# Stacks of query and key parts made by ordinary matmuls with an identity instead of transpose-mode matmuls

## The chip, the core and the metric

The kernel runs on one core of a Trainium2 chip. The metric is the device time of one execution in microseconds (us); the number given for the kernel before is the median of three runs. One execution was also recorded by the hardware profiler, and all rows below come from that recording.

The core has five engines that work side by side, each through its own list of instructions in a fixed order: TensorE (PE) for matrix products, VectorE (DVE), ScalarE (ACT), GpSimd (POOL) and SyncE (SP), which here only starts transfers. An instruction waits until what it reads is there and until the buffer that it writes is free; everything behind it on the same engine waits with it.

## What is computed

The reference is a decoder trunk of two layers over 512 tokens with 1024 features, in float32. Each layer has three kinds of attention heads that share one input projection, and then a SwiGLU feed-forward part:

```
h = rms_norm(x);  p = h @ w_in                       # one projection, columns shared out
o_fox  = softmax(q k^T / 8 + c[t] - c[s]) v          # 6 forgetting heads of 64
o_diff = (softmax(q1 k1^T) - lam softmax(q2 k2^T)) v # 4 differential heads, q and k 2 x 32
score[t, s] = sum_h w[t, h] relu(qi[t, h] . ki[s])   # indexer, 4 heads of 64
sel = the topk best causal keys of each query by score
o_dsa  = softmax over sel of q k^T / 8, times v      # 6 sparse heads, one shared key and value
x = x + concat(o_fox, o_diff, o_dsa) @ w_out
x = x + (silu(gate) * up) @ w_down                   # gate, up = rms_norm(x) @ w_gate_up
```

All attention is causal. The kernel keeps the best 128 keys of each query (`topk` is a quarter of the 512 tokens) by a mask: keys that are not selected get a large bias.

## The kernel before

**Tiles.** Tokens go in four blocks of 128. Products that must be accurate are made from two parts of each operand, a high part rounded to float32r and the rest as a second float32r number; `mm3` multiplies high by high, low by high and high by low. A score of a forgetting or sparse head needs no `mm3`: the parts are laid next to each other along the feature axis, as [high | low], and a product over 128 rows has several of the terms at once. For that, the parts of queries and keys, which lie with tokens on the partitions, are turned round so that features lie on the partitions. This is what `stacked` does: it takes four blocks of [128 tokens, 128 part-features], turns each by one PE instruction with the 128x128 identity `identr` into a quarter of one PSUM tile `tp_...`, and lets ACT copy the tile to SBUF as `T_...`. In the instruction the block is the operand that is loaded into PE (a weight load, PEld in the trace), and the identity is the one that moves through.

There are 96 such stacks in the kernel, 48 in each layer, so 384 instructions: 4 indexer queries, 2 indexer keys and 2 shared keys (named `tp_iq`, `tp_ik`, `tp_sk`); 4 for each of the 4 differential heads (`tp_qd`, `tp_kd`); 3 for each of the 6 forgetting heads (`tp_qf`, `tp_kf`); 1 for each of the 6 sparse heads (`tp_qs`).

**Stages.** A layer begins with the projections and the indexer scores. Then the heads go through rounds: in round r the probabilities of head r are transposed (L450, tile `t_...`), head r + 1 is scored (L432, tile `s_...`), and head r - 1 weighs its values (L476, L482, L483, tile `o_...`), with units of projection work (L172 to L174, `mm3`, tile `pj`) laid between the stages. The differential heads come first, then the forgetting ones, then the sparse ones. Scores go from PSUM through a DVE reduction with the bias (L438, reads `s_...`, writes `x_...` and the row minimum `st_...`) and an ACT exponential (L439).

**The search.** Meanwhile DVE selects the best keys of each query: `top_keys` runs 16 rounds over three query blocks, and each round and block is a MAX (L831, the eight best of the row) and a MATCH_REPLACE (L832, which takes them out). These 96 steps per layer are called steps of the search below; three instructions (L835) turn the result into biases for the sparse heads. A tile `top0_3_8` is that of layer 0, block 3, round 8.

**What sets the order.** PE's order is that of the program text (the tables `ORDER`, `FILL` and `SEARCH` interleave the generators). The order of each other engine is set at build time by a scheduler, which keeps its own account of when each instruction could begin and picks among those that are ready by priority. Priorities come from the order of the text and are raised or lowered for some kinds of work by the table `AHEAD` (`"topk": 150` for the search, `"ttr": 1000` for the reductions of scores, `"stack": 60` for the copies out of the stacks). On the chip each engine then follows that fixed list.

**Buffers.** The PSUM tiles `tp_...`, `s_...`, `t_...` and a few small ones share four buffers (tag `st`). A PE instruction that writes such a tile waits until the reader of the tile that had this buffer four tiles earlier is through; for a score tile that reader is the DVE reduction L438.

Of the kernel before, what the change touches and what calls it, by code (L numbers as in the profile page):

```python
# [31 lines left out]
# Rounds of the heads: the order of the stages of each round; the units of projection work and the  # L32
# steps of the search for the best keys that follow each stage.
# [16 lines left out]
INDEX_FILL = "03210121000201021"  # units of projection work between the stages of the indexer  # L50
# by how much the scheduler prefers (or, below zero, puts off) a kind of work
# [6 lines left out]
# products of probabilities and values, for the pairs of the differential and forgetting heads and for  # L58
# the sparse heads: 4 in float32, 2 from parts
# [3 lines left out]
# Column chunks of the input projection: indexer queries; indexer key, shared key and value, gates;  # L63
# then query-key pairs and values of the differential and forgetting heads, and the sparse queries.
# [22 lines left out]
def trunk(ctx: ExitStack, tc: tile.TileContext, x_in, w_in, w_out, w_gu, w_dn, vecs, gfeat, rope, out):  # L87
# [21 lines left out]
    # ---- residual stream, feature-major: x[m][p, t] = x[t, 128 m + p]  # L109
# [4 lines left out]
    # ---- constants  # L114
# [6 lines left out]
    tri = const.tile([P, P], F32, name="tri")  # tri[s, t] = s <= t  # L121
    G.affine_select(out=tri, in_=ones, compare_op=ALU.is_ge, fill=0.0, base=0,
                    pattern=[[1, P]], channel_multiplier=-1)
    # causal[:, 384 - 128 i:] is the mask of query block i over its 128 (i + 1) keys
    causal = const.tile([P, S], F32, name="causal")
    cdiag = causal[:, S - P:]  # 0 where key <= query, else BIG
# [10 lines left out]
    # rope tables: [blk, 16] cos|cos, -sin|sin for 64-wide heads; [blk, 8] for 32-wide ones  # L137
# [5 lines left out]
    # values of a pair of heads and of the sparse heads: high | low  # L143
# [4 lines left out]
    # ---- weights: load, and split exactly into two 12-bit parts  # L148
    def weights(src, n, step, name, eng=V, load=None):
        """Parts (high, low) of n columns, as a function of the column slice."""  # L150
# [25 lines left out]
    def rsqrt(m, name, out=None):  # L176
        """m ** -0.5: a first value from the scalar engine, then a Newton step."""
        shape = list(m.shape)
        y = small.tile(shape, F32, tag="rs_y", name=f"rsy_{name}")
        t = small.tile(shape, F32, tag="rs_t", name=f"rst_{name}")  # L180
        A.activation(y, m, AF.Ln)
        A.activation(y, y, AF.Exp, scale=-0.5)
        e = V
        e.tensor_tensor(t, y, y, op=ALU.mult)
        e.tensor_tensor(t, t, m, op=ALU.mult)
        e.tensor_scalar(t, t, -0.5, 1.5, op0=ALU.mult, op1=ALU.add)
        e.tensor_tensor(out, t, y, op=ALU.mult)

    def split_input(l, which, ms):
        """Parts of x * g for feature tiles ms."""  # L190
# [12 lines left out]
    def square_sum(pool, name):  # L203
        """Sum over feature tiles of x * x."""
# [8 lines left out]
    def token_rms(acc, name):  # L213
        """1 / rms per token, token-major [P, NB]."""
# [9 lines left out]
    def attention(l, ap):  # L224
        """The attention half of layer l; on the tensor engine the stages of three heads overlap,
        with units of the projections in between."""
# [5 lines left out]
        # ---- small per-layer vectors  # L232
# [8 lines left out]
        # ---- projection of one chunk of columns, token-major  # L241
        def project(c, start=False):
            """Yields after each unit of the tensor engine's work; returns one [P, n] per token block.
            At the start a unit is a feature tile, not a token block."""
# [24 lines left out]
        # the first chunks go half by half, so that the last feature tiles of y may come late  # L269
        p_iq, p_ik, p_dq = project(C_IQ, l == 0), project(C_IK), project(C_DQK0)  # L270

        def step(gen, n):
            """n units of gen; what it returned, once it is through."""
            for _ in range(n):
                try:
                    next(gen)
                except StopIteration as e:
                    return e.value
# [36 lines left out]
        # ---- token-major inputs of the heads  # L315
        def head_norm(raw, nh, d, name):
            """raw [P, NB, nh, d] times 1 / rms over d, in place."""
# [23 lines left out]
        def split_hl(raw, hl, hi=False):  # L341
            """raw [P, NB, n, d] into hl [P, NB, n, 2, d]: high | low."""
# [3 lines left out]
        def split_hlh(raw, hl):  # L346
            """raw [P, NB, n, d] into hl [P, NB, n, 3, d]: high | low | high."""
# [4 lines left out]
        def split_values(src, dh, dl, b, mode):  # L352
            """Projected values of token block b into their parts."""
# [50 lines left out]
        # ---- stacks of transposes  # L404
        def stacked(src, name, tag="qk", bufs=5):
            """Transposes of src(b) [P, 128] for all token blocks, as one [128, S] tile."""
            ps = st_tile(f"tp_{name}", F32R)
            for b in range(NB):
                T.transpose(ps[:, b * P:(b + 1) * P], src(b), identr)
# [7 lines left out]
        def key_stacks(hl, name, tag="qk", bufs=5):  # L417
            """hl(b) [P, 3, 64] of a key head -> its [high; low] and [low; high] stacks."""
            return [stacked(lambda b: flat(hl(b))[:, 64 * e:64 * e + 128], f"{name}{e}", tag, bufs) for e in range(2)]

        # ---- scores, probabilities, weighted values of one head
        def scores(blocks, q, k, bias, p, stat, name):
            """Per query block: p = exp(logits - max), with the sums; q holds negated queries."""
# [17 lines left out]
        def transposed(blocks, p, parts, name, mode):  # L441
            """Probabilities of the query blocks, transposed into parts [keys, queries]."""
# [9 lines left out]
            for i in blocks:  # L452
                # key block j of query block i goes to POFF[j] + 128 (i - j)
# [16 lines left out]
        def weigh(js, o, parts, val, mode):  # L470
            """o += [high | low]^T P^T for key blocks js; the lower half is to be added to the upper one."""
# [15 lines left out]
        def broadcast_rows(cols, n, name):  # L487
            """cols [P, NB, n], token-major -> rows [n, S] in DRAM."""
# [10 lines left out]
        def out_parts(kt, osb, wide, name, g=None):  # L499
            """Parts of a pair's output osb times its rows, or times wide (token-major) and g (per feature)."""  # L500
# [13 lines left out]
        class Head:  # L514
            """One head of a pair. split, stack: its parts and their transposes; score, trans, pv by
            blocks; fin, oss, rows: the pair's output, after its second head."""
# [11 lines left out]
            def split_(self):  # L528
                pr, h = self.pr, self.h
                if self.kind == "d":  # L530
                    raw = raws["d", pr]
                    # queries high|high|low|low, keys high|low|high|low: one product has all four terms
# [48 lines left out]
            def biases(self, blocks):  # L581
                """What is added to the negated logits: the mask; for forgetting heads, the gates as well."""
# [15 lines left out]
            def score(self, blocks):  # L598
# [7 lines left out]
                else:  # L606
                    V.reciprocal(rr[self.pair][:, lo:hi, self.h], st[0][:, 4 + lo:4 + hi])
                    # p1 / s1 - lam p2 / s2 = (p1 - lam (s1 / s2) p2) / s1
# [57 lines left out]
            def row_factors(self):  # L666
                """The factors of both heads as rows over the tokens, on all partitions of a head."""
# [11 lines left out]
            def oss(self):  # L679
                """rms norm over each differential head's 64 features"""  # L680
# [24 lines left out]
        # ---- indexer, shared key and value, gates  # L705
# [19 lines left out]
        # gates: log sigmoid, cumulative sum over tokens  # L725
# [23 lines left out]
        # ---- what the tensor engine does between the stages of the heads  # L749
# [53 lines left out]
        # ---- indexer scores  # L803
# [8 lines left out]
        def index_score(h, q, i):  # L812
            """Adds head h to the scores of the causal keys; -BIG for the others."""
# [11 lines left out]
        def top_keys():  # L825
            """The TOPK best keys of each query: the others get the bias BIG."""
# [25 lines left out]
        # ---- the heads: in round r, head r is transposed, head r + 1 scored, head r - 1 weighs its values  # L852
# [34 lines left out]
    def feed_forward(l, fp):  # L887
# [4 lines left out]
        def gate_up(f, between=None):  # L892
            """The f-th tile of gate and up, before the norm."""
# [50 lines left out]
        for f in range(2, NF):  # L944
            activate(f, gate_up(f))
            # each group of the down projection follows once its inputs had time to arrive
# [7 lines left out]
    with tc.manual_schedule(engines={mybir.EngineType.PE}):  # L954
        # the tensor engine reaches its full clock while the first loads are under way
# [70 lines left out]
```

## Time and profile before

| | |
|---|---|
| median of three runs | 1309.02 us (1307.33 to 1311.05) |
| span of the profiled execution | 1310.7 us |
| PE busy | 1273.4 us, 97% of the span |
| PE weight loads (beside PE) | 1083.1 us |
| DVE busy | 809.8 us |
| ACT busy | 657.2 us |
| POOL busy | 245.0 us |
| mean granted clock of PE | 0.993 of full speed |

The profiled execution lies 1.7 us above the median. The layers' attention halves fill about 0 to 280 us and 690 to 930 us; the feed-forward halves follow each, and there PE hardly stops.

In a row of the timeline the columns are the start (us from the span's start), the duration in us, engine, line, operation, output and inputs, and shapes; "x4" means four instructions of that form in a row merged into one line, and a bracket at the end gives idle time before it and what ended that. Matmuls are pipelined: a row's duration is from entry to the end of the last result, and the next instruction starts long before. The time that one costs PE is the distance from its start to the next start.

### The profile page before, as it was taken

How to read it: one execution, taken by the hardware profiler on the slowest of the kernel's cores; microseconds unless marked ns; L12 is line 12 of the kernel's file. 1: busy time of each engine (PE TensorE's matmuls, PEld its weight loads, DVE VectorE, ACT ScalarE, POOL GpSimd, SP SyncE). 2: the span in 40 equal slices, each digit the busy share in tenths (PEclk: the TensorE clock that was granted, in tenths of full speed). 3: DMA queues.
4: the chain of work that ended last, by engine and by line, in shares of the span. 5: the costliest groups of instructions: out<-in, count | busy, mean ns of one | idle time of the engine just before them, and what ended most of it. 6: DMA issues, size and time to landing. Idle time of an engine off the chain costs nothing. (4 is left out here: it accounts for less than half of the span.)

```text
span 1310.7 us, 19466 instructions
## 1 busy us (share of the span) xinstructions
PE 1273.4 (97%) x7058; PEld 1083.1 (83%) x7058; DVE 809.8 (62%) x1833; ACT 657.2 (50%) x1514; POOL 245.0 (19%) x269
## 2 busy tenths in 40 slices
PE   9989999999999999999999899989899999999998
PEld 9988796777888888888899888968778888888887
DVE  5699996865444444444546999868745534544442
ACT  6668777854332233232456786768533323333321
POOL 2454464220000000000025535642100000000000
PEclk9999999999999999999999999999999999999999
DMA  5221121123333333333322212211323333333332
GB/s 182 88 90 42 53 81 36 59 81 97 98 97 97 97 97 89 97 95 98 93 86 82 73 50 65 62 53 54 94 88 97 97 97 97 97 90 107 95 93 99
DMA packets 35495, 112.62 MB, mean 86 GB/s; under 512 B 4024, under 2 KB 4552, under 8 KB 35400
## 3 DMA queue, kind: packets, MB, share of 16 engines
q1 hardware_dynamic: 35400, 111.38, 28.7%
q8 instruction: 56, 0.92, 0.3%
q14 instruction: 39, 0.32, 0.1%
HBM read 109.19 MB, written 2.17 MB: 85 GB/s over the span
## 5 line engine op out<-in xcount | busy, mean ns | idle before, releaser
L172 PE MATMUL gu<-yh,wh_gu 128*128 128x512 f32 x704 | 274.4, 390 | 3.3 <-DVE gs L909 3.3
L174 PE MATMUL gu<-yl,wh_gu 128*128 128x512 f32 x704 | 273.9, 389 | 0.0
L173 PE MATMUL gu<-yh,wl_gu 128*128 128x512 f32 x704 | 273.9, 389 | 0.0
L159 ACT ACTIVATE wh_gu<-raw_gu 128x512 fp32r<-128x512 f32 x176 | 111.2, 632 | 253.7 <-PE gu L174 211.8
L172 PE MATMUL pj<-wh_in,yh 128*128 128x256 f32 (+1 forms) x704 | 202.0, 287 | 0.7 <-ACT wh_in L159 0.7
L174 PE MATMUL pj<-wl_in,yh 128*128 128x256 f32 (+1 forms) x704 | 199.2, 283 | 0.2 <-DVE wl_in L162 0.2
L173 PE MATMUL pj<-wh_in,yl 128*128 128x256 f32 (+1 forms) x704 | 199.2, 283 | 0.2 <-DVE yl L199 0.2
L162 POOL TENSOR_TENSOR wl_in<-raw_in,wh_in 128x512 fp32r<-128x512 f32 x72 | 99.7, 1402 | 488.9 <-ACT wh_in L159 484.8
L162 DVE TENSOR_TENSOR wl_gu<-raw_gu,wh_gu 128x512 fp32r<-128x512 f32 x176 | 121.8, 692 | 109.4 <-ACT wh_gu L159 106.7
L172 PEld LDWEIGHTS gu<-yh,wh_gu 128*128 128x128 f32 x704 | 132.2, 188 | 31.0 <-DVE gs L909 3.7
L174 PEld LDWEIGHTS gu<-yl,wh_gu 128*128 128x128 f32 x704 | 132.1, 188 | 27.7
L173 PEld LDWEIGHTS gu<-yh,wl_gu 128*128 128x128 f32 x704 | 132.2, 188 | 27.2
L172 PE MATMUL dn<-gh,wh_dn 128*128 128x512 f32 x352 | 138.7, 394 | 0.0
L174 PE MATMUL dn<-gl,wh_dn 128*128 128x512 f32 x352 | 138.0, 392 | 0.0
L159 ACT ACTIVATE wh_dn<-raw_dn 128x512 fp32r<-128x512 f32 x96 | 57.3, 597 | 159.5 <-PE dn L174 111.5
L172 PEld LDWEIGHTS pj<-wh_in,yh 128*128 128x128 f32 x704 | 134.7, 191 | 2.6 <-issue 1.2
L173 PE MATMUL dn<-gh,wl_dn 128*128 128x512 f32 x352 | 136.6, 388 | 0.0
L173 PEld LDWEIGHTS pj<-wh_in,yl 128*128 128x128 f32 x704 | 135.0, 192 | 1.1 <-DVE yl L199 0.4
L174 PEld LDWEIGHTS pj<-wl_in,yh 128*128 128x128 f32 x704 | 135.1, 192 | 0.4 <-DVE wl_in L162 0.4
L162 DVE TENSOR_TENSOR wl_dn<-raw_dn,wh_dn 128x512 fp32r<-128x512 f32 x96 | 62.2, 648 | 68.5 <-ACT wh_dn L159 67.6
L174 PEld LDWEIGHTS dn<-gl,wh_dn 128*128 128x128 f32 x352 | 66.1, 188 | 15.5
L173 PEld LDWEIGHTS dn<-gh,wl_dn 128*128 128x128 f32 x352 | 66.1, 188 | 14.8
(301 smaller groups left out, 2153.8 us busy)
## 6 DMA issues: line engine op xcount, KB each, us to landing
raw_gu<-in_w_gu SPq DMA_DIRECT2D x88, 512.0 KB
raw_in<-in_w_in SPq DMA_DIRECT2D x39, 512.0 KB
raw_dn<-in_w_dn SPq DMA_DIRECT2D x32, 448.0 KB
raw_dn<-in_w_dn SPq DMA_DIRECT2D x16, 512.0 KB
cr<-rtd_c SPq DMA_DIRECT2D x12, 256.0 KB
raw_o_fox<-in_w_out SPq DMA_DIRECT2D x8, 384.0 KB
raw_o_dsa<-in_w_out SPq DMA_DIRECT2D x8, 384.0 KB
x<-in_x_in SPq DMA_DIRECT2D x8, 256.0 KB
```

Source lines behind the costliest of these rows:

```text
L159: A.activation(h[:, :w], raw[:, o:o + w], AF.Copy)
L162: eng.tensor_tensor(lo[:, :w], raw[:, o:o + w], f32(h[:, :w]), op=ALU.subtract)
L172: T.matmul(ps, ah, bh, start=first, stop=False, skip_group_check=True)
L173: T.matmul(ps, al, bh, start=False, stop=False, skip_group_check=True)
L174: T.matmul(ps, ah, bl, start=False, stop=last, skip_group_check=True)
```

## The change

In `stacked`, the four instructions are issued as matmuls of float32r operands with `start` and `stop` set instead of as transposes, and the PSUM tile is declared float32 instead of float32r. Operands, shapes, tile, buffers and the copy behind them are the same. A product of a block with an identity gives the block, turned round. Comments were removed from the text as well, and one blank line came in, so that lines from 410 on have a number larger by one.

```
         def stacked(src, name, tag="qk", bufs=5):
-            """Transposes of src(b) [P, 128] for all token blocks, as one [128, S] tile."""
-            ps = st_tile(f"tp_{name}", F32R)
+
+            ps = st_tile(f"tp_{name}")
             for b in range(NB):
-                T.transpose(ps[:, b * P:(b + 1) * P], src(b), identr)
+
+                T.matmul(ps[:, b * P:(b + 1) * P], src(b), identr, start=True, stop=True)
             dst = ap.tile([P, S], F32R, tag=tag, name=f"T_{name}", bufs=bufs)
```

PE's list has the same 6419 rows in the same order, 384 of them in the new form. The lists of the other engines hold the same instructions in another order: 278 of DVE's 1727 rows stand elsewhere, 134 of ACT's, 10 of POOL's and 4 of SP's. Most of what moved on DVE is the search.

DVE's list of the kernel before, at the first score reduction of the first forgetting head (`x_f0_0_00_0` is layer 0, pair 0, head 0, query block 0; MAX and MATCH_REPLACE are steps of the search):

```order
L831 MAX top0_3_8_2800<-sc0_3_687 128x8
L831 MAX top0_1_9_2817<-sc0_1_685 128x8
L832 MATCH_REPLACE sc0_3_687<-top0_3_8_2800,sc0_3_687 128x512
L832 MATCH_REPLACE sc0_1_685<-top0_1_9_2817,sc0_1_685 128x256
L831 MAX top0_2_9_2904<-sc0_2_686 128x8
L831 MAX top0_3_9_2907<-sc0_3_687 128x8
L438 ISA x_f0_0_00_0_2168,st_f0_0_00_2029<-s_f0_0_00_0_2163,fbf0_0_0_0_2146 128x128
```

The same place in DVE's list of the changed kernel:

```order
L832 MAX top0_2_12_3167<-sc0_2_686 128x8
L833 MATCH_REPLACE sc0_1_685<-top0_1_12_3164,sc0_1_685 128x256
L833 MATCH_REPLACE sc0_2_686<-top0_2_12_3167,sc0_2_686 128x384
L832 MAX top0_3_12_3173<-sc0_3_687 128x8
L832 MAX top0_1_13_3176<-sc0_1_685 128x8
L832 MAX top0_2_13_3179<-sc0_2_686 128x8
L833 MATCH_REPLACE sc0_3_687<-top0_3_12_3173,sc0_3_687 128x512
L439 ISA x_f0_0_00_0_2168,st_f0_0_00_2029<-s_f0_0_00_0_2163,fbf0_0_0_0_2146 128x128
```

Before, the search is in its round 9 when the reduction's turn comes, with 58 of the 96 steps done; now it is in round 13, with 80 done. In layer 1 the same two counts, 58 and 80, stand at `x_f1_0_00_0`.

DVE's list of the kernel before, at the first reduction of the next head, `x_f0_0_10_0` (`pt1` is the low part of transposed probabilities, `hk` and `ss` belong to the inputs of later heads):

```order
L832 MATCH_REPLACE sc0_3_687<-top0_3_11_3138,sc0_3_687 128x512
L831 MAX top0_1_12_3164<-sc0_1_685 128x8
L831 MAX top0_2_12_3167<-sc0_2_686 128x8
L832 MATCH_REPLACE sc0_1_685<-top0_1_12_3164,sc0_1_685 128x256
L832 MATCH_REPLACE sc0_2_686<-top0_2_12_3167,sc0_2_686 128x384
L325 TENSOR_REDUCE ss_f0_2_2355<-sq_f0_2_2_2359 128x8
L438 ISA x_f0_0_10_0_2384,st_f0_0_10_2289<-s_f0_0_10_0_2379,fbf0_0_1_0_2304 128x128
```

The same place in DVE's list of the changed kernel:

```order
L833 MATCH_REPLACE sc0_3_687<-top0_3_15_3247,sc0_3_687 128x512
L469 TENSOR_TENSOR pt1_f0_0_0_2271<-t_f0_0_0_2_2327,pt0_f0_0_0_2270 128x128
L836 TENSOR_SCALAR sc0_1_685<-sc0_1_685 128x256
L836 TENSOR_SCALAR sc0_2_686<-sc0_2_686 128x384
L836 TENSOR_SCALAR sc0_3_687<-sc0_3_687 128x512
L299 TENSOR_SCALAR gd1_7111<-vec1_6800 128x32
L300 COPY gd1_7111<-vec1_6800 128x32
L313 TENSOR_TENSOR nlam1_7124<-ls1_7119,le1_7122 128x1
L740 MEMSET before1_7749 128x6
L439 ISA x_f0_0_10_0_2384,st_f0_0_10_2289<-s_f0_0_10_0_2379,fbf0_0_1_0_2304 128x128
```

Here the count goes from 76 steps to all 96, and the three closing instructions of the search and four small ones have come ahead of the reduction as well. No instruction has moved from ahead of these two reductions to behind them.

On POOL, half of the low part of one weight chunk (`wl_in0_7_0`) now stands behind three instructions that it stood ahead of, which make biases of the first forgetting head (`fbf`). On ACT, copies that make the query parts of a differential head (L540) now stand ahead of the copy of a key stack (L412). On SP, the load of one weight chunk (`raw_in0_6_0`) now stands behind the loads of gate rows (`cr`).

## Rows read from the trace of the kernel before

**Rows 1.** Stretches: length; busy (count) of PE, PEld, DVE, ACT, POOL; PE clock; DMA:

```profile
68.00:190.00 122.00, 113.33 (x865) 102.17 (x865) 121.23 (x387) 91.98 (x263) 58.99 (x67) 0.99 0.21 66
719.00:811.50 92.50, 86.95 (x654) 77.38 (x653) 92.08 (x302) 72.66 (x205) 44.99 (x45) 0.98 0.21 62
```

**Rows 2.** Waits of DVE, 68 to 168 us: total us, times, longest:

```profile
DVE ss_f L325 <- ACT sq_f L323: 0.4, 1, 0.4
```

**Rows 3.** Timeline of DVE up to the first forgetting reduction (value loads left out):

```profile
145.90 1.01 DVE L831 MAX8 top<-sc 128x8 f32<-128x512 f32 x2
...
146.89 0.67 DVE L832 MATCH_REPLACE8 sc<-top,sc 128x512 f32<-128x512 f32 x1
...
147.56 0.40 DVE L832 MATCH_REPLACE8 sc<-top,sc 128x256 f32<-128x256 f32 x1
147.88 1.14 DVE L831 MAX8 top<-sc 128x8 f32<-128x384 f32 x2
148.94 0.27 DVE L438 CUSTOM_DVE_ANT_0 x_f<-s_f,fbf 128x128 f32<-128x128 f32 x1
```

**Rows 4.** Timeline of PE behind that reduction, layer 0 and layer 1:

```profile
149.61 0.62 PE L432 MATMUL s_f<-T_kf,T_qf 128*128 128x384 f32 x2 [1.21 <-DVE st_f L438]
...
798.08 0.62 PE L432 MATMUL s_f<-T_kf,T_qf 128*128 128x384 f32 x2 [1.22 <-DVE st_f L438]
```

**Rows 5.** Timeline of POOL and PE around one weight part that moves on POOL:

```profile
85.91 1.29 POOL L162 TENSOR_TENSOR wl_in<-raw_in,wh_in 128x512 fp32r<-128x512 f32 x1
...
87.61 0.86 POOL L590 TENSOR_SCALAR fbf<-cr,ncum 128x512 f32<-128x512 f32 x1
...
92.84 0.28 PE L174 MATMUL pj<-wl_in,yh 128*128 128x256 f32 x1
```

**Rows 6.** A weight load of `stacked` (ns min/median/max), and the timeline of twelve of its transposes:

```profile
L409 PEld LDWEIGHTS tp_ik<-identr,hlik x16: 138/140/143, 41.8 to 693.6; 128*128 128x128 f32 x16
...
41.87 0.80 PE L409 MATMUL tp_ik<-identr,hlik 128*128 128x128 f32 x8
42.50 0.50 PE L409 MATMUL tp_iq<-identr,hliq 128*128 128x128 f32 x4
42.84 0.35 PE L172 MATMUL pj<-wh_in,yh 128*128 128x256 f32 x1
43.03 0.28 PE L173 MATMUL pj<-wh_in,yl 128*128 128x256 f32 x1
```

**Rows 7.** Ordinary float32r products: load (busy us, mean ns), timeline of 202 moving columns:

```profile
L172 PEld LDWEIGHTS pj<-wh_in,yh 128*128 128x128 f32 x704 | 134.7, 191 | 2.6 <-issue 1.2
...
29.89 0.27 PE L174 MATMUL pj<-wl_in,yh 128*128 128x202 f32 x1
30.00 0.28 PE L172 MATMUL pj<-wh_in,yh 128*128 128x202 f32 x1
```

**Rows 8.** Timeline: a short float32r product, and eight plain float32 ones with their successor:

```profile
239.77 0.22 PE L482 MATMUL o_s<-pt_s,svals 128*128 128x128 f32 x1
239.83 0.22 PE L483 MATMUL o_s<-pt_s,svals 128*64 128x128 f32 x1
...
120.88 2.37 PE L476 MATMUL o_d<-pt_d,vals 128*64 128x512 f32 x8
123.18 0.33 PE L450 MATMUL t_d<-ident,p_d 128*128 128x128 f32 x1
```

**Rows 9.** Later waits of PE, layer 0 (168 to 280 us), layer 1 (811.5 to 930 us):

```profile
PE wo_dsa L172 <- ACT oh L510: 3.0, 1, 3.0
...
PE s_s L432 <- DVE st_s L438: 1.1, 1, 1.1
...
PE wo_dsa L172 <- ACT oh L510: 3.5, 1, 3.5
PE s_s L432 <- DVE st_s L438: 2.3, 1, 2.3
```

**Rows 10.** Stretch of PE at half clock behind a wait (columns as in rows 1):

```profile
151.78:155.19 3.41, 3.41 (x23) 3.41 (x21) 3.41 (x12) 2.72 (x8) 1.94 (x3) 0.50 0.00 0
```

## The prediction

> **What bounds the kernel now.** I began with busy time by stretch, then the waits, then the timeline at the places where a wait ends. Between 68 and 190 us, in the attention half of layer 0, the reader should see two engines close to full: PE busy for 113.33 of 122.00 us and DVE for 121.23; in layer 1 the same stage has DVE busy for 92.08 of 92.50 us [rows 1]. A full DVE need not be the bound, since a filler (the search) may be what fills it. The waits decide that: DVE has one wait of 0.4 us in a hundred microseconds [rows 2], while PE stops for DVE: the score product at 149.61 us waited 1.21 us for the score reduction L438 to release its buffer, and the one at 798.08 in layer 1 1.22 us [rows 4]. So here PE runs at DVE's pace, and what stands ahead of such a reduction in DVE's list delays PE, microsecond for microsecond. Outside these stages PE is the bound and stops seldom: after 168 us the long waits are for the outputs of sparse heads (3.0 and 3.5 us) and for a sparse score reduction (1.1 and 2.3 us) [rows 9].
>
> **Part 1: the product itself.** 384 transposes become ordinary products. A run of twelve goes from 41.87 to 42.84 us, 0.97 us, and the product behind it holds PE 0.19 us until 43.03 [rows 6] where such a product takes 0.11 to 0.12: with this 0.07 us the run costs 1.04 us, 0.087 us each. Their weight load takes 140 ns, that of an ordinary float32r product 191 [rows 6, 7]. The trace has no ordinary float32r product with 128 loaded and 128 moving columns. The nearest row is that with 202 moving columns: 29.89 to 30.00, 0.11 us from start to start [rows 7]; the load, not the 202 columns, should be what sets it, so I take 0.11 for 128 columns too: +0.024 us each. Bound below: a 128-column product that is followed by one with 64 loaded columns took 0.06 us [rows 8], which would be a gain of 0.025. Bound above: eight plain float32 products, two each with 512, 384, 256 and 128 moving and 64 loaded columns, took 2.30 us from 120.88 to 123.18 [rows 8], which is 0.115 us for every 128 moving columns; doubled for 128 loaded columns instead of 64, an estimate of 0.22 us, +0.13 each.
>
> 384 x 0.024 = 9.2 us of work on PE. What of it is on the path? Per layer 32 transposes stand before 68 us and 68 after 168 us, where PE is the bound; 92 stand in the stage that DVE bounds, where 8.7 us of PE are free [rows 1] and 92 x 0.024 = 2.2 us fits. So 2 x 100 x 0.024 = **+4.8 us**. With the cover gone it would be 4.4 more.
>
> A page of the Trainium skill speaks against the change: "Perfetto Trace Analysis", section Transposes, asks for transpose over a standard matmul, since a transpose skips arithmetic, and "TensorE: Matmul & The Clock Gate", section Terms, puts transpose mode at 4x faster for FP32. By that an ordinary product would cost 4 x 0.087 = 0.35 us, and 200 of them on the path +52 us, about 1383 with part 2 (an estimate). No run here shows the ordinary form on these operands; the row of 0.11 us, on float32r operands, does not agree with it.
>
> **Part 2: DVE's order.** The diff touches PE alone, but the lists of the other engines come out in another order, and DVE's is the one that matters. Ahead of the reduction of the first forgetting head stand 80 steps of the search where 58 stood, in both layers, and nothing has moved out from ahead of it. Price of a step: from 145.90 to 148.94 us DVE does six, with their value loads, and nothing else (two MAX, two MATCH_REPLACE, two MAX), 3.04 us, 0.507 each [rows 3]. 22 x 0.507 = 11.1 us. DVE has no idle time ahead of that reduction to take them in (the wait of 0.4 us comes later, for an L325 behind it) [rows 1, 2], so it begins at about 160.0 instead of 148.94, and the product that waits for it has no slack: it already waits 1.21 us [rows 4]. PE therefore resumes 11.1 us later, in layer 1 as well (wait 1.22) [rows 4].
>
> Is it given back? At the next head's reduction all 96 steps stand ahead where it was 76: 20 x 0.507 = 10.1 us, with seven small instructions behind them, so DVE is still that late. Behind it DVE no longer has any search to do and is early; but PE then has to do all its remaining work, which is as much as before, and can only regain what it waited. Those waits follow PE's own products (scores, then reduction, exponential, transpose; sparse outputs at the end) and move with them. So nothing comes back, and the term is 2 x 11.1 = **+22.3 us**.
>
> **Part 3: other lists.** On POOL, half of a low weight part goes behind three instructions that make forgetting biases. It ran at 85.91 for 1.29 us, the longest of the three takes 0.86 us (at 87.61), and PE needs it at 92.84 [rows 5]: 5.6 us of room cover at most 3 x 0.86 = 2.6 us; if the room were gone, 2.6 us would be the price. On SP one weight load goes behind the loads of gate rows; its parts are due still later, and the same 5.6 us bounds what a late chunk could be worth. On ACT two copies of query parts go ahead of a key stack; the score behind it would be late by about a microsecond, but its reduction stands behind the longer list on DVE, and this is hidden there. I take zero, with up to 3 us in the range. PSUM's tile type changes nothing in bytes or buffers.
>
> The sum against the profiled execution: 1310.7 + 22.3 + 4.8 = 1337.8 us of span; the median stands 1.7 us lower, so **1336**.
>
> **The clock.** Behind the wait at 149.61 PE was granted 0.50 of full speed, 1.2 instead of 2.4 GHz, for 3.41 us, with PE busy all through [rows 10]. A stretch of that kind loses about 1.7 us. Longer or additional waits in the same stage may bring one or two more per layer: up to 2 x 2 x 1.7 = 6.8 us, which I keep for the upper end, not in the sum. The wait that is there now brings one already.
>
> **Rivals.**
>
> *The moved search is absorbed.* If PE had work in hand that doesn't depend on DVE, or if DVE's list before held the same steps elsewhere ahead of the reduction, only the products would count: 4.8 to 9.2 us, 1314 to 1318. It decides at the wait before 149.61: if PE waits no longer there, this holds. Against it: PE follows the text's order and cannot pull anything forward, and the wait is already above zero [rows 4].
>
> *Faster: the search's early end takes waits away.* DVE would be free from about 180 us on, and the waits that PE now has later, 3.0 + 1.1 + 3.5 + 2.3 = 9.9 us [rows 9], would vanish, while the moved steps cost nothing: 1309.0 + 4.8 - 9.9 = 1304. It needs the reduction at 148.94 to start no later than now; from there on each step ahead of it eats a half microsecond of the gain, so some ten steps per layer decide. Against it: 22 steps stand there, and the two longest of these waits are for ACT.
>
> *An ordinary product costs as a plain float32 one.* +0.13 x 200 = 26 us on the path, and 92 x 0.13 = 12 us per layer in the DVE stage, over the 8.7 us of room by 3.3: 1309.0 + 22.3 + 26 + up to 6.6 = 1357 to 1364. For it: the upper bound; against it: the operands are float32r, as in [rows 7].
>
> *The change does nothing on PE* (the product is carried out as before, 0.087 us each): the order on DVE is still the new one, 1331.
>
> **How the numbers follow.** Forecast 72%: with product costs from -0.01 to +0.05, some give-back (up to 2 us per layer) and up to four more stretches at 1.2 GHz it spans 1327 to 1347. Absorbed, wholly or by half (to 1320): 12%. Faster rival 3%. Plain float32 price 5%. Nothing on PE 2%. Further stalls beyond 1347 (DVE against POOL, ACT's two copies): 6%. The range from 1318 to 1347 leaves out most of the absorbed case, the faster one, the float32 price and the stalls, about 20%. A measurement of this kernel tells 0.3% (3.9 us) from no change: faster 3%; within it 4% (absorbed, with products at their cheap end); slower 93%.
>
> **What would show it.** In the changed kernel's trace: weight loads of `stacked` near 190 ns rather than 140 and 0.11 us from start to start; PE's busy sum up by about 9 us; the first forgetting reduction at about 160 us instead of 148.94, in layer 1 the same shift; a wait of PE for `st_f` or `st_d` L438 several microseconds longer between 95 and 170 us, or several such waits that add up to 11; DVE without gaps until then, the search over near 170 to 180 us, and idle time of DVE behind it. The lists of PE's work after 280 us should take as long as before. I am wrong if that reduction comes no later than 152 us, if PE has regained its lag by 280 us, or if the products cost other than 0.06 to 0.22 us.

## The result and the profile after

The changed kernel takes **1338.47 us** (median of 4 runs, 1337.61 to 1341.57) where the kernel before took 1310.03 in the same comparison: a ratio of **1.0227** (95% interval 1.0203 to 1.0250). The two medians are 28 us apart (their quotient is 1.0217); by the ratio, which the table below goes by, the loss is 30 us. The forecast was 1336, in a range from 1318 to 1347. The time is where it was said to be; the experiments show that two terms of the sum were not what they seemed, and that the close agreement is partly luck.

The page of the changed kernel, span and engines, beside 1310.7 us, PE 1273.4 and DVE 809.8 before (this profiled execution is the slowest of the four, 3.1 us above the median):

```profile
span 1339.8 us, 19460 instructions
PE 1296.9 (97%) x7058; PEld 1101.7 (82%) x7058; DVE 806.0 (60%) x1833; ACT 658.9 (49%) x1514; POOL 236.8 (18%) x269
```

The span grew by 29.1 us. PE's busy time grew by 23.5 us and its idle time (span less busy) from 37.3 to 42.9, by 5.6. That is the first surprise: a delay by DVE ought to stand in PE's idle time.

First the products. A weight load of `stacked`, and twelve of the new products in the timeline of PE (start, duration):

```profile
L410 PEld LDWEIGHTS tp_kf<-identr,hk_f x96: 186/192/192, 153.7 to 889.7; 128*128 128x128 f32 x96
...
42.98 1.00 PE L410 MATMUL tp_ik<-identr,hlik 128*128 128x128 f32 x8
43.82 0.61 PE L410 MATMUL tp_iq<-identr,hliq 128*128 128x128 f32 x4
44.27 0.33 PE L172 MATMUL pj<-wh_in,yh 128*128 128x256 f32 x1
44.44 0.28 PE L173 MATMUL pj<-wh_in,yl 128*128 128x256 f32 x1
```

The load went from 140 to 192 ns. Twelve products take 1.29 us, where twelve transposes took 0.97 [rows 6]. The product behind them holds PE 0.17 us (44.27 to 44.44) where such a product takes 0.12; with these 0.05 us the run costs 1.34 us, 0.112 each, against 0.087 for a transpose. So +0.025 us each, where +0.024 was forecast from a row with 202 columns.

Then DVE's timeline up to the first reduction of a forgetting head, in layer 0 and in layer 1, and the PE product that waits for it in layer 0:

```profile
159.35 0.67 DVE L833 MATCH_REPLACE8 sc<-top,sc 128x512 f32<-128x512 f32 x1
159.95 0.28 DVE L439 CUSTOM_DVE_ANT_0 x_f<-s_f,fbf 128x128 f32<-128x128 f32 x1
...
825.31 0.27 DVE L439 CUSTOM_DVE_ANT_0 x_f<-s_f,fbf 128x128 f32<-128x128 f32 x1
...
160.63 0.44 PE L433 MATMUL s_f<-T_kf,T_qf 128*128 128x384 f32 x1 [0.42 <-DVE st_f L439]
```

The reduction begins at 159.95 instead of 148.94 [rows 3], 11.0 us later, and the product at 160.63 instead of 149.61 [rows 4], 11.0 later too. PE's lag, the start of a product here less the start of the same product before, is 14.0 us at the end of layer 0's attention half (292.10 before, 306.10 now), and 27 to 29 from 827 us to the end of layer 1's: nothing is given back. But the product's wait has not grown; it fell from 1.21 to 0.42 us. Where PE's lag went instead, the stretches of the first stage show (columns as in rows 1; 102.39 to 109.22 and 805.50 to 815.70 lie ahead of those two reductions):

```profile
68.00:190.00 122.00, 110.48 (x782) 98.10 (x782) 116.29 (x380) 83.75 (x237) 52.78 (x61) 0.94 0.20 59
719.00:811.50 92.50, 82.94 (x588) 73.76 (x587) 82.52 (x266) 66.17 (x186) 35.91 (x36) 0.95 0.20 60
...
102.39:109.22 6.83, 5.12 (x23) 5.13 (x24) 6.65 (x28) 4.46 (x17) 0.07 (x1) 0.50 0.00 0
805.50:815.70 10.20, 9.45 (x33) 6.93 (x34) 8.24 (x33) 6.11 (x19) 0.83 (x1) 0.50 0.00 1
```

PE was granted 1.2 instead of 2.4 GHz in eleven stretches of 3.41 us (37.5 us) where the kernel before had five (17.1 us, one of them [rows 10]); a stretch that begins in the last 2 us of either span is left out. At half clock a projection product of 256 columns takes 0.21 us from start to start, at full clock 0.12:

```profile
105.01 0.41 PE L174 MATMUL pj<-wl_in,yh 128*128 128x256 f32 x1
105.22 0.41 PE L172 MATMUL pj<-wh_in,yh 128*128 128x256 f32 x1
```

The longer work fills time in which PE would have waited; this is my reading, not shown by itself, and not all of it: in the run search_back below, with five such stretches as before, PE's busy time still grew by 13.7 us (to 1287.1) and its idle time by 1.8. In the changed kernel 20 us more at half clock account for up to 10 us of the 23.5 us by which PE got busier (an estimate), the products for 384 x 0.024 = 9.2 us; the remaining 4 are not assigned. DVE, gapless before [rows 1, 2], now has gaps: from the first step of the search to the first forgetting reduction it idles 4.0 us, before it was 0.2. Its longest waits from 68 to 160 us:

```profile
DVE x_d L439 <- PE s_d L433: 2.0, 1, 2.0
DVE raw_d L339 <- POOL rb_d L338: 1.5, 1, 1.5
```

DVE waits for PE (this wait ends at 111.36 us, behind the first two stretches at half clock), and for a rope part on POOL.

### The profile page after: what moved, and what is told of

Its sections match the earlier page's. It is cut to its first block, busy times and chain, and to the rows that moved or that the text cites. A ratio compares the mean times of both kernels' runs of the same rounds, so it can differ in the third digit from the quotient of the medians.

```text
span 1339.8 us, 19460 instructions
## 1 busy us (share of the span) xinstructions
PE 1296.9 (97%) x7058; PEld 1101.7 (82%) x7058; DVE 806.0 (60%) x1833; ACT 658.9 (49%) x1514; POOL 236.8 (18%) x269
## 4 chain that ended last, share of the span: by engine, by line
PE 75%; DVE 15%; DMA 4%; ACT 3%; issue 2%; POOL 1%; SPq 0%; DVEq 0%; ACTq 0%; POOLq 0%
PE gu L172 12%; PE gu L173 12%; PE gu L174 12%; PE dn L172 6%; PE dn L174 6%; PE dn L173 6%; PE pj L172 4%; PE pj L173 4%; PE pj L174 4%; DVE sc L833 3%; DVE top L832 3%; DMA rw_s<-rtd_s 2%; DVE x_d L439 1%; DMA rw_f<-rtd_f 1%; PE wo_dsa L172 1%
## 5 line engine op out<-in xcount | busy, mean ns | idle before, releaser
L172 PE MATMUL pj<-wh_in,yh 128*128 128x256 f32 (+1 forms) x704 | 205.0, 291 | 0.6 <-ACT wh_in L159 0.6
L173 PE MATMUL pj<-wh_in,yl 128*128 128x256 f32 (+1 forms) x704 | 201.9, 287 | 0.0
L162 POOL TENSOR_TENSOR wl_in<-raw_in,wh_in 128x512 fp32r<-128x512 f32 x72 | 96.6, 1357 | 512.7 <-ACT wh_in L159 486.7
L172 PEld LDWEIGHTS pj<-wh_in,yh 128*128 128x128 f32 x704 | 138.2, 196 | 2.5 <-issue 1.2
L173 PEld LDWEIGHTS pj<-wh_in,yl 128*128 128x128 f32 x704 | 138.4, 197 | 0.7
L174 PEld LDWEIGHTS pj<-wl_in,yh 128*128 128x128 f32 x704 | 137.9, 196 | 0.2 <-DVE wl_in L162 0.2
```

The source lines that it names most:

```text
L162: eng.tensor_tensor(lo[:, :w], raw[:, o:o + w], f32(h[:, :w]), op=ALU.subtract)
L172: T.matmul(ps, ah, bh, start=first, stop=False, skip_group_check=True)
L173: T.matmul(ps, al, bh, start=False, stop=False, skip_group_check=True)
L174: T.matmul(ps, ah, bl, start=False, stop=last, skip_group_check=True)
```

## The experiments

The lists of the four other engines can be set apart from the products. In the runs below every instruction of DVE, ACT, POOL and SP is tied behind its neighbour in a chosen list, with an order-only edge (issue order, no wait; lines of these kernels are numbered 4 higher than in the kernel before, so that L436 there is L432). With the transposes and the lists of the kernel before, this gives the same program as before, instruction for instruction. The edit, the same in all twelve runs but for the table `QUEUES` and for whether `stacked` has transposes or products:

```
                 feed_forward(l, fp)
+    traced = {i.name: i for i in tc.nc.cur_bb.bb.instructions}
+    for queue in QUEUES:                     # one list of instruction numbers for each engine
+        seen = [f"I-{k}" for k in queue if f"I-{k}" in traced]
+        for earlier, later in zip(seen, seen[1:]):
+            tc.add_manual_dep(traced[later], earlier, mybir.DependencyInfo(
+                mybir.DependencyClass.NoSync, mybir.DependencyReason.DATA), reason="order")
```

The theory was that of the prediction: the moved search makes the loss. What was measured, all against the kernel before on the same chip; "lists" says whose order the engines follow, "reduction" is the start of the first forgetting reduction in layer 0 in the profiled execution, "at 1.2" the number of 3.41-us stretches of PE at half clock:

| run | products | search | other DVE, ACT | POOL, SP | ratio (95% interval) | us | reduction | at 1.2 |
|---|---|---|---|---|---|---|---|---|
| kernel before | no | old | old | old | 1 | 0 | 148.94 | 5 |
| changed kernel | yes | new | new | new | 1.0227 (1.0203 to 1.0250) | +30 | 159.95 | 11 |
| products_old_lists | yes | old | old | old | 0.9982 (0.9967 to 0.9997) | -2 | 148.24 | 3 |
| the same again | yes | old | old | old | 0.9993 (0.9979 to 1.0007) | -1 | 151.87 | 3 |
| transposes_new_lists | no | new | new | new | 1.0175 (1.0147 to 1.0202) | +23 | 157.93 | 11 |
| search_alone2 | no | new | old | old | 1.0208 (1.0187 to 1.0230) | +27 | 160.64 | 13 |
| search_half | no | half | old | old | 1.0095 (1.0075 to 1.0115) | +12 | 155.69 | 8 |
| search_back | yes | old | new | new | 1.0158 (1.0136 to 1.0180) | +21 | 154.15 | 5 |
| dve_act_rest_new | yes | old | new | old | 1.0131 (1.0095 to 1.0166) | +17 | 151.11 | 7 |
| pool_sp_new | yes | old | old | new | 1.0031 (1.0015 to 1.0047) | +4 | 150.91 | 5 |

(us: ratio less one, times 1310.)

### Products or order

> Ordinary products as in the changed kernel, but DVE, ACT, POOL and SP issue in exactly the order of the kernel before. Theory (the moved search makes the loss): only the products on the path are left, +4.8 us, 1313 to 1318; the first forgetting reduction stays within 2 us of 148.9. Rival (the products themselves make most of the loss, by their loads, their time or the clock): at least 1325. Rival (ordinary products cost nothing beside the load): 1309.

> Transposes as before, but DVE, ACT, POOL and SP issue in exactly the order of the changed kernel. Theory: +22.3 us, 1329 to 1335, the first forgetting reduction at about 160 instead of 148.9. Rival (the products make the loss): below 1315. Together with the run of ordinary products under the old lists it should add up to the whole loss of 28 us; if both are small, the two parts need each other.

The products under the old lists cost nothing: -2 us, and -1 when the run was repeated. The new lists with the old transposes cost 23 us, within a microsecond of the term in the prediction (22.3). So the loss is the order, which the scheduler chose anew because of the products; the products alone would have been free. The two do not add up to the whole: products cost -1 to -2 us under the old lists and, by the two ratios, about 7 under the new ones (0.5%, each ratio known to 0.25%). Under the new lists both variants have eleven stretches at half clock, and PE's busy time differs by 9.7 us (1287.2 and 1296.9), about the 9.2 us of the products, while its idle time differs by 2 (44.9 and 42.9): little hides them there. Under the old lists PE's busy time grew by 4.3 us in the first run (1277.7 against 1273.4) and by 8.0 in the repeat (1281.4), and its idle time fell from 37.3 to 29.6 and 30.7. So most of the added work went into waits that were there anyway. Both runs had three stretches at half clock instead of five, which by the estimate above gives back up to 3.4 us; how much of the products' low cost comes from that, no run separates.

### The search by itself

> Transposes as before and all lists as before, except that the steps of the search stand as far ahead in DVE's list as in the changed kernel (80 instead of 58 ahead of the first forgetting reduction). Theory: the same as with all new lists, within 4 us, 1328 to 1335. Rival (the moves on ACT, POOL and SP, or of other DVE instructions, carry it): below 1320.

It took 1.0265 (1.0237 to 1.0293), +35 us, more than with all new lists. The trace shows that the run was not what it was meant to be: the first step of the search began at 82.95 us instead of 68.22, since the list let no step start before all twelve score updates were through, and then the steps stood packed ahead of early reductions. PE waited longer for score reductions than in any other run:

```profile
PE s_d L436 <- DVE st_d L442: 25.5, 6, 8.6
```

So it tells only that packed steps cost more. The same with that mended, and with half the distance:

> Transposes and all lists as before, only the steps of the search stand where they stand in the changed kernel relative to the other DVE instructions (31 instead of 24, 58 instead of 40 and 80 instead of 58 ahead of three reductions); other than in the first try of this, a step may start as soon as the scores of its own query block are complete, as in both kernels, so that the search begins at 68 us and not at 83. Theory: as with all new lists, 18 to 27 us above the kernel before. Rival (the first try's 35 us are the true price of the search, and other moves in the new lists win a part back): 30 to 37 us above. Rival (the other moves carry the loss): less than 10 above.

> As the run before, but each step of the search moves only half as far (69 instead of 58 or 80 ahead of the first forgetting reduction). Theory (PE runs at DVE's pace with no slack, 0.5 us a step): half of that run's loss, 9 to 14 us above the kernel before. Rival (a threshold: some steps fit in without loss): less than 6. Rival (the loss comes from the clock that falls at any longer wait): nearly all of it, above 16.

22 steps cost 27 us in the two layers, 11 steps 12 us: proportional, 0.6 us for a step that DVE takes 0.5 us for [rows 3]. Neither slack nor a threshold shows. At half the distance the reduction stands between the two ends:

```profile
155.69 0.28 DVE L442 CUSTOM_DVE_ANT_0 x_f<-s_f,fbf 128x128 f32<-128x128 f32 x1
```

### The search put back

> The changed kernel with ordinary products and its lists for ACT, POOL, SP and all of DVE except that the steps of the search are put back to where they stand in the kernel before (58 ahead of the first forgetting reduction). Theory: the loss is gone, -4 to +5 us against the kernel before. Rival (the other moves or the products carry a good part under these lists): 10 us or more above.

This is where the theory failed. With the search back at 58 steps the loss is still 21 us. The waits of PE between 60 and 170 us in that run:

```profile
PE s_d L436 <- DVE st_d L442: 2.7, 1, 2.7
PE t_d L454 <- DVE p_d L626: 1.9, 1, 1.9
PE s_d L436 <- ACT T_kd L416: 1.1, 1, 1.1
```

The second is new: PE waits for a combination of probabilities of a differential head (`p_d`, L622 of the kernel before). DVE's timeline there, first before, then with the search put back, and POOL's in the latter:

```profile
92.39 0.34 DVE L611 SCALAR_TENSOR_TENSOR st_d<-st_d,nlam,st_d 128x1 f32<-128x1 f32 x2
92.65 1.27 DVE L622 SCALAR_TENSOR_TENSOR p_d<-p_d,st_d,p_d 128x384 f32<-128x384 f32 x2
```

```profile
94.42 1.20 DVE L615 SCALAR_TENSOR_TENSOR st_d<-st_d,nlam,st_d 128x1 f32<-128x1 f32 x2
95.55 2.36 DVE L626 SCALAR_TENSOR_TENSOR p_d<-p_d,st_d,p_d 128x384 f32<-128x384 f32 x2
```

```profile
94.18 1.44 POOL L546 TENSOR_TENSOR hq_d<-raw_d,hq_d 128x256 fp32r<-128x256 f32 x2 [2.67 <-ACT hq_d L544]
95.56 1.28 POOL L166 TENSOR_TENSOR wl_in<-raw_in,wh_in 128x512 fp32r<-128x512 f32 x1
```

The same four instructions take 3.5 us (94.42 to 97.91) instead of 1.5 (92.39 to 93.92), because under the new lists they meet two TENSOR_TENSORs of POOL (the last part of this section returns to such meetings). Ahead of that DVE had waited 1.11 us at 87.05 for a rope part on POOL (`raw_d`, L343, waiting for `rb_d`), whose addition stands four score reductions earlier in DVE's new list. Two more runs split what is left:

> Ordinary products, the search where it stands in the kernel before, POOL and SP with the lists of before; ACT and the rest of DVE with the lists of the changed kernel. The run with all new lists but the old search lost 20 us, which the theory of the search alone does not explain. New theory (small changes of order among head inputs and combinations on DVE and ACT delay the transposes of probabilities that PE waits for at 93 and 744 us): the 20 us are all here, 16 to 24 above the kernel before. Rival (the moved weight part on POOL and the moved load on SP): less than 6 above.

> Ordinary products and DVE and ACT with the lists of before; POOL and SP with the lists of the changed kernel. Theory (DVE and ACT carry it): as with the products under the old lists, -4 to +4 against the kernel before. Rival (POOL's list holds up DVE or a weight part): 8 or more above.

ACT and the rest of DVE carry +17 us, POOL and SP +4; against the products under the old lists (-2) that is 19 and 6, 25 together, about the 23 that the search put back still lost. In the last one DVE's instructions other than the search took 52.0 us instead of 50.2 from the first step to the reduction, and DVE idled 1.1 instead of 0.2, and PE waited 1.12 us at a place where it had not waited at all:

```profile
106.48 0.66 PE L413 MATMUL tp_qd<-identr,hq_d 128*128 128x128 f32 x4 [1.12 <-DVE st_d L442]
```

Behind it PE ran at 1.2 GHz from 108.5 to 112 us. ACT's list and the rest of DVE's were not tried apart, so which instruction of the two carries most of the 17 us is open.

So three edits of the lists, each alone, cost 27 us (with transposes), 19 and 6 (with products), and all together 23 with transposes and 32 with products: far less than their sum of 52. No run has the transposes with the other new lists and the old search, so a part of the 19 and 6 may be the products, which cost 8 to 9 us more under all new lists than under the old ones. The reading that fits is that they delay the same reductions, so that a longer delay covers part of the others. PE's lag bears it out in layer 0. At the product that begins at 103.61 us before (the first of a `tp_qd`) the lag is 7.9 us in the changed kernel, 4.5 with the search alone, 5.9 with the search put back; at the score product of 149.61 it is 11.0, 11.7 and 5.2. (Each of these has 1.1 to 1.3 us in it that are there at 10 us.) Between the two the moved search by itself adds 7.2 us, but only 3.1 in the changed kernel, which the other lists had already made late.

### Putting the search off

> Transposes and lists as before, except that the search is put off: 49 instead of 58 steps ahead of the first forgetting reduction, 20 instead of 24 and 34 instead of 40 ahead of two earlier ones, the last steps among the instructions ahead of the sparse heads. Theory (PE runs at DVE's pace there, and the search sets it): PE's waits for score reductions between 68 and 168 us (2.4, 1.2, 0.6 us) and their like in layer 1 shrink, 1299 to 1305. Rival (these waits are latency and not DVE's list): 1307 to 1311. Rival (the steps that are left push later reductions): above 1312.

1.0016 (1.0001 to 1.0031), no gain. The reduction did come 2.4 us earlier, at 146.56, and in layer 1 3.3 earlier (794.13 against 797.40). The gain was lost behind 168 us, where the steps put off stand ahead of work for the sparse heads; PE's waits there, of which the second is new:

```profile
PE wo_dsa L176 <- ACT oh L514: 2.9, 1, 2.9
PE rt_f L494 <- ACT sq_s L327: 2.4, 1, 2.4
PE t_f L454 <- ACT p_f L443: 2.0, 2, 1.9
```

> Ordinary products with the lists of before, and a tenth of the search's steps put off (52 instead of 58 ahead of the first forgetting reduction), the last ones into idle stretches of DVE ahead of one late forgetting reduction and of one output product (195 and 214 to 218 us). Theory: the gain of the earlier try (the first forgetting reduction 2.4 us earlier, in layer 1 3.3) without what it lost behind 190 us, together with the products under the old lists: 5 to 9 us below the kernel before. Rival (the waits only move to the next place): 1 to 4 below, as with the products alone.

1.0013 (1.0001 to 1.0026): no gain either, against the kernel before or against the products alone (0.9982 and 0.9993). The reduction came at 149.62, after a search that began at 69.94. Neither of the two later places of the search gained anything.

### Small instructions beside POOL

What is left is why DVE needed less time for the same other instructions in the changed kernel. From the first step of the search to the first forgetting reduction DVE spent, by its rows:

| | search | other 171 | idle | began | reduction |
|---|---|---|---|---|---|
| before, layer 0 | 29.3 | 51.2 | 0.2 | 68.2 | 148.9 |
| changed, layer 0 | 40.1 | 45.8 | 4.0 | 70.0 | 159.9 |
| before, layer 1 | 29.4 | 48.4 | 0.2 | 719.4 | 797.4 |
| changed, layer 1 | 40.2 | 46.2 | 4.8 | 734.1 | 825.3 |

The search cost 10.9 us more, as forecast (11.1); the other instructions cost 5.4 and 2.2 less. To see by how much an instruction was late, I take its time (start to next start) less that of the same instruction where it meets no TENSOR_TENSOR of POOL, in seven of the traces. In layer 0 of the kernel before, eleven took over 0.3 us more, 9.5 us in all, and every one of them began while POOL ran a TENSOR_TENSOR; in the changed kernel there were four, 3.3 us. All that began so, small excesses too, add up to 9.5 and 4.0 us, in layer 1 to 6.6 and 4.1: differences of 5.5 and 2.4 where 5.4 and 2.2 are to be explained. One of the eleven, with the POOL instruction that it met (before; duration in the second column):

```profile
140.43 0.99 DVE L184 TENSOR_TENSOR rst_d<-rsy_d 128x8 f32<-128x8 f32 x1
...
138.40 3.00 POOL L162 TENSOR_TENSOR wl_in<-raw_in,wh_in 128x512 fp32r<-128x512 f32 x2 [8.37 <-ACT wh_in L159]
```

An instruction on 128x8 elements, 0.16 us elsewhere, lasts 0.99 and ends at 141.42, when the second of the two POOL instructions in its row ends (138.40 + 3.00 = 141.40). The page "SBUF — State Buffer" of the Trainium skill, section "SBUF: two separate sides", says that DVE and GpSimd share one pair of ports, which an instruction holds to its end, and that a DVE instruction with two inputs in SBUF needs it while GpSimd reads there; the trace agrees (0.99 us, ended 0.02 us behind POOL).

> Ordinary products with all lists of before, but on DVE eight small instructions (four in each layer, of 0.07 us where nothing else runs), which took 0.4 to 1.2 us because they began while POOL ran a TENSOR_TENSOR and ended when that ended, change places with the one to three steps of the search behind them. Theory (a step of the search does not wait for POOL, such an instruction does): they fall to at most 0.2 us, the other instructions of DVE ahead of the first forgetting reduction take 2 to 4 us less in each layer, the reduction comes 1.5 to 3.5 us earlier, and PE regains what it waits for DVE there, 1 to 4 us in all. Rival (POOL delays whatever DVE runs beside it): the time of the search grows by as much. Rival (the stalls move to the next instruction): nothing changes.

> The same kernel as the first run (ordinary products, all lists of before), beside the run with the small instructions moved. Theory: again 0 to 4 us below the kernel before; the stretches at 1.2 GHz are again fewer than the five of the kernel before if the products are what keeps the clock up, about five if their number was chance.

Eight such instructions, four in each layer, took 6.8 us in all under the old lists and 3.7 with one to three steps of the search moved ahead of them (four of them still 0.6 to 0.9 us each). The same instruction as above, with ordinary products in both kernels (first with the lists of before, then moved):

```profile
143.34 0.99 DVE L188 TENSOR_TENSOR rst_d<-rsy_d 128x8 f32<-128x8 f32 x1
```

```profile
141.42 0.16 DVE L188 TENSOR_TENSOR rst_d<-rsy_d 128x8 f32<-128x8 f32 x1
```

The time of the search stayed at 29.3 us: its steps do not wait for POOL. The gain per layer was smaller than expected, though (the other instructions 1.9 us less in layer 0, 0.4 in layer 1), because some met the next POOL instruction. The kernel takes 0.9981 (0.9965 to 0.9997) of the kernel before, 2.5 us less; against the same kernel without the move (0.9993, 0.9979 to 1.0007) it is not told apart. The repeat of the first run had three stretches at half clock again.

## Why the prediction was right, and where it was not

**The order of the search: right in its place, near in its size.** DVE's list sets the pace, the reduction begins 11.0 us later where 11.1 was forecast, a step of the search costs about half a microsecond, and half the steps cost half. With transposes all new lists cost 23 us where the sum had 22.3, but the search by itself costs 27 (24 to 30 by its interval).

**But the 11 us are not made only of search steps.** In layer 0 they are +10.9 for the steps, -5.4 for fewer meetings with POOL, +3.8 of new gaps on DVE, and +1.8 of lag that PE brought from before 68 us (1.1 of it is there at 10 us, ahead of the first stack; the 32 products make about 0.8); in layer 1 +10.8, -2.2, +4.6 and 14.7 of lag, 27.9 together. The step that failed is that what stands ahead of such a reduction in DVE's list delays PE "microsecond for microsecond": DVE's list had no idle time, but its instructions had 9.5 us of hidden waiting in them, counted as busy. And 7.9 of the 11.0 us of PE's lag were there at 103.61 us already, 5.9 with the search put back. The tight agreement is partly luck.

**The products: right price, wrong path.** +0.024 us each was right. That 200 of them lie bare on the path, +4.8 us, was not: under the old lists they cost nothing (-2 and -1 us). PE's waits in the whole span, before and then with products under the old lists (engine line <- engine line: us in all, times, longest):

```profile
PE s_d L432 <- DVE st_d L438: 4.0, 4, 2.1
PE s_s L432 <- DVE st_s L438: 3.4, 2, 2.3
PE t_f L450 <- ACT p_f L439: 3.3, 4, 1.5
```

```profile
PE s_d L436 <- DVE st_d L442: 2.6, 4, 1.0
PE s_s L436 <- DVE st_s L442: 2.3, 2, 1.2
PE t_f L454 <- ACT p_f L443: 1.5, 4, 0.6
```

They shrank by 4.3 us in all: PE arrived later, and others were no later. So PE also waits where I took it for the bound. Under the new lists the same products cost about 7 us. By the rule of "TensorE: Matmul & The Clock Gate", section Terms, in the Trainium skill, transpose mode is 4x faster for FP32; on these float32r operands the runs show 0.087 against 0.11 us, 1.3 times and not 4.

**The other lists: zero was wrong, and hidden.** I looked at a weight part on POOL, a load and two copies, and found cover for each. What I passed over were moves among head inputs on DVE and ACT (a rope addition ahead of four reductions is one), 19 us with the products and the old search, and POOL's instructions as something that small ones of DVE run into, 6 us with SP's. Which moves carry most of the 19 is open: three moves were weighed, where 134 of ACT's rows stand elsewhere. In the changed kernel their cost is hard to see, because the search delays many of the same reductions; DVE's new gaps (1.5 us for the rope part alone) are a trace of it. The bound of 3 us for them was off by a factor of five or more (25 us, or 16 without what the products may have in it); the rival with the search absorbed would not have given 1314 but some 1331 (1.0158 times 1310).

**The clock.** I kept up to four more stretches at 1.2 GHz for the upper end; there were six more. They also undo one of the signs that I named: PE's waits for DVE did not grow by 11 us (between 68 and 170 us from 5.9 to 7.6), which I put down to PE's work at half clock. A lag is better read from the starts of the same instruction in both traces than from the waits.

**Nothing comes back: right.** The lag of 11.0 us at the first forgetting reduction is 14.0 at the end of the layer's attention half. The rival in which an early search frees DVE for later is out: the search ends at 174 us, and from 168 to 300 us PE's wait for a sparse score reduction fell from 1.1 to 0.3 us, but waits for `pt_f` and `pt_s` on DVE came instead (1.2 and 0.5), and the longest, for ACT's sparse outputs, went from 3.0 to 3.2.

## What to carry to other kernels

A change to one instruction can be free and still cost 2%, when a scheduler orders other engines anew because of it: compare the lists of every engine, and look for what now stands ahead of the instruction that the bound engine waits for. Then pin the old order and run the change without the reordering; it tells in one run which of the two to mend. And when two edits delay the same instruction, taking one away shows the other: price each alone before calling one the cause.

## What the runs showed of the hardware

A DVE instruction of 0.15 to 0.21 us (`rst_d` and `om_d` on 128x8, `ss_f` on 128x16, `st_d` on 128x2) lasted up to 1.3 us when it began beside a POOL TENSOR_TENSOR, and ended 0.01 to 0.03 us behind POOL's (141.42 against 141.40 above). Not every instruction does: in the kernel before, 2 RECIPROCALs, 3 TENSOR_REDUCEs and 16 score reductions ahead of the first forgetting reductions of both layers began beside one with at least 0.5 us to go and were not stretched; MAX and MATCH_REPLACE did not stretch (29.2 to 29.4 us for 58 steps ahead of the reduction in layer 0, in every kernel with the old search, however many meetings it had). The trace counts this as busy time.

PE at half clock can hide waits: in the changed kernel PE ran at 1.2 GHz in eleven stretches of 3.41 us instead of five, and its idle time grew by 5.6 us in a span that grew by 29.1. Kernels with ordinary products under the old lists had three such stretches or two, in all three profiles; the kernel before with transposes had five, and with transposes and a search put off five again. With products and a search put off there were four, with products and POOL's and SP's new lists five. Whether it is the products that keep the clock up, or the waits that they fill, no run here separates.
